# Two-layer sparse-attention trunk on one core: first gate summed by VectorE, compression's products and the second layer's values in longer runs, second scale and shift in four column tiles

## The chip, the core and the metric

The kernel runs on one core of one Trainium2 chip. TensorE (PE in the profile; PEld is its weight load), VectorE (DVE), ScalarE (ACT), GpSimd (POOL) and the queue engine SyncE (SP) each run their own queue of instructions in order and wait for each other by semaphores. The metric is the device time of one execution in microseconds (us), lower is better.

## The reference

Two transformer blocks over x (256 tokens, 1024 wide). c is one row of 1024 numbers; it gives each layer a shift, a scale and a gate. Layer 0 uses `nsa_mixer` (three attention branches, one of them over compressed blocks), layer 1 uses `moba_mixer` (with 256 tokens it is one causal attention). Everything is float32.

```python
cond = silu(c)
for i in range(2):
    shift, scale, gate = split(cond @ ada_w[i] + ada_b[i], 3)          # 1024 -> 3 x 1024
    h = rms_norm(x, norm_g[i]) * (1 + scale) + shift
    y = nsa_mixer(h, ...) if i == 0 else moba_mixer(h, ...)
    x = x + gate * y
# in nsa_mixer, for keys (i = 0) and values (i = 1):
#   flat: 15 blocks x 4 heads of 32 tokens x 64 = 2048 numbers each
#   gelu(flat @ cmp_w1[i] + cmp_b1[i]) @ cmp_w2[i]                     # cmp_w1: 2048 x 256
# attention, per head: softmax(q @ k.T * scale, causal) @ v;  y = (o * silu(z)) @ w_out
```

## The kernel before

Weights come through SP's queue into 128x1024 buffers (`early`, then six `raw`). Large products are made of two halves: ScalarE rounds a weight piece to float32r (`hi`), VectorE subtracts it from the piece (`lo`), and TensorE adds hi.hi, hi.lo and lo.hi. HT holds the normed input, KTA the keys, VA the values, qg the queries, GT the gated outputs. Small sums are plain float32; each is two instructions of TensorE in the trace.

The program is written in its natural order, and a planner (`Plan.issue`) sets the real one: it keeps a clock for each engine, picks the ready operation that can start first, then by level and by key, and allots buffers. Two tables move single operations by hand: `LATER_BY` shifts keys (operation numbers), `HOLD` gives an earliest start in planned ns. Operations recorded in one `plan.group()` are issued together. All recorded operations carry the line of the issuing helper (L404), so the profile's groups go by tile names.

Some products use column tiles: with `tile_position=(0, 32*j)` a product with 32 output rows takes a quarter of the array's columns, with `(0, 64*e)` a half, and products in different tiles run side by side. The four places that matter here:

- `ada_rows` / `ada_gate(0)`: the first layer's gate row is cond @ ada_w, 16 products of 32 rows x 512 columns in four column tiles (`ps<-raw,condz`), spread to all partitions by two products with ones (`ps<-row,ones`). `ada_gate(1)` does the second one on VectorE (`gate<-raw,condz,gate`, 8 sums of 128x1024) and spreads it by two full-width products (`ps<-gate,ones`).
- `ada_ss(1, 0, 4)` and `ada_ss(1, 4, 4)`: the second layer's scale and shift, 16 such products each, then four transposes each (`ps<-identF,row`).
- `cmp_steps`: the compression's products, 16 groups of two products of 64 rows x 256 columns (`ps<-p,p`), one half of the columns for keys and one for values. Its weights lie in `p` buffers.
- `values`, called by `pair_b` for each of the second layer's eight head pairs (`ps<-pT,VA`).

The first three are handed out as side work: `beside()` takes a step of the list `side` between steps of the attention.

Of the kernel before, what the change touches and what calls it, by code (L numbers as in the profile page):

```python
# [1 line left out]

# [12 lines left out]
OP = mybir.AluOpType  # L15
AX = mybir.AxisListType

P = 128
S = 256
D = 1024  # L20
HEADS = 16
KVH = 4
HD = 64
# [11 lines left out]

TICK = 10240 / 3
DEEP = 2e4
TILED, LATER, PAUSE = -0.5, 0, 93.0
SHORT_ROWS, SMALL, BEHIND, EARLY_RATE = 1.1, 7e4, 5500.0, 348.0
ISSUE, FIRST_BYTE, RATE, LANDED = 450.0, 1500.0, 315.0, 700.0  # L40

LATER_BY = [
# [12 lines left out]
]  # L55
SHIFT = {i: d for a, b, d in LATER_BY for i in range(a, b + 1)}
HOLD = {
    29: 2400, 32: 3700, 33: 3700, 51: 7200, 312: 35600, 391: 48800, 1276: 152700, 1340: 169100, 1350: 168000,
    1415: 182100, 1573: 197400, 1576: 198800, 1579: 197400, 1585: 198700, 1636: 205200, 1655: 209300,
}  # L60


# [10 lines left out]
class Plan:  # L73
# [120 lines left out]
    def _cost(self, engine, method, args, kw, aps):  # L194
        def free(a):
            n = 1
            for _, k in a.ap[1:]:
                n *= k
            return n

        if "dma" in method:
            self.bytes = free(aps[0]) * aps[0].shape[0] * 4
            if aps[1].shape[-1] <= 128 and self.bytes > 1e5:
                self.bytes *= SHORT_ROWS
            if self.bytes <= 1e5:
                self.bytes += SMALL
            return max(ISSUE, self.bytes / RATE) if engine == "S" else ISSUE
        psum = any(str(a.space).endswith("PSUM") for a in aps)
        n = max(free(a) for a in aps)
        if engine == "T":  # L210
            if method == "transpose":
                return 262.0 if aps[1].dtype == F32 else 180.0
            cols = free(aps[2])
            if aps[2].dtype == F32:
                m, rows = free(aps[1]), aps[1].shape[0]
                if "tile_position" in kw and m * rows <= 64 * P:
                    return max(cols * 4.28 * max(32, m) / P * max(32, rows) / P, 60.0) + (100.0 if rows < P else 0.0)
                return 2 * max(cols * 2.14, 264.0)
            return max(cols * (1.07 if aps[2].dtype == F32R else 1.0), 264.0)
        if engine == "A":  # L220
            return 0.833 * n + (51.0 if psum else 94.0) + 93.0 * sum(isinstance(kw.get(k), bass.AP) for k in ("bias", "scale", "accum_out"))
        if engine == "G":
            return 1.5 * n + 270.0
        if method == "reciprocal":
            return 6.5 * n + 68.0
        fast = not psum and (method == "tensor_copy" or method.startswith("tensor_scalar"))
        pointers = len(aps) - 2 if method.startswith("tensor_scalar") else 0
        return (0.521 if fast else 1.042) * n + 68.0 + 61.0 * pointers
# [22 lines left out]
    def issue(self, opening=()):  # L251
# [51 lines left out]
        while done < len(ops):  # L303
            best = None
            for e, ops_e in ready.items():
# [4 lines left out]
                for op in ops_e:  # L310
# [4 lines left out]
                    for n in op["needs"]:  # L315
# [4 lines left out]
                        t = max(t, r)  # L320
# [41 lines left out]
            if e == "T":  # L362
                tick = int(start // TICK)
                if op["mode"] != mode:
                    cost += 240.0
                mode = op["mode"]
                cost = cost * (1 / 2.4 if tally.get(tick - 1, 0.0) >= 3060.0 else 1 / 1.2)
                tally[tick] = tally.get(tick, 0.0) + op["cost"]
                if (start + cost) // TICK > tick:
                    cost += PAUSE  # L370
# [61 lines left out]
def kernel(  # L432
# [39 lines left out]
        late["pool"] = ctx.enter_context(tc.tile_pool(name="attn", bufs=1))  # L472

    KP = 2
    W1_HOME = ("p", "p")
    SPINS = 8
    START = [("s", 2, 2), ("k", 1), ("s", 4, 2), ("k", 2), ("s", 6, 2), ("k", 3)]
    plan.tag("acc", psum, 512, 2, space="PSUM")
# [155 lines left out]
    def load(src, tag="raw"):  # L634

        t = tile_of(tag, *src.shape[1:])
        with plan.at(CHAIN):
            Q.dma_start(t, src)
        return t
# [54 lines left out]
    def ada_ss(l, k0, nk, loaded=None):  # L694
# [23 lines left out]
        V.scalar_tensor_tensor(a_, a_, 1.0, RT[:, ROW_G + 8 * l + k0:ROW_G + 8 * l + k0 + nk], op0=OP.add, op1=OP.mult)  # L718
        V.tensor_add(b_, tv[:, :, 0], RT[:, b:b + nk])

    gates_of = {}

    def ada_gate(l):

        gate = gates_of[l] = tile_of("gate", D)
        bias = bass.AP(tensor=ada_b.tensor, offset=ada_b.offset + l * 3 * D + 2 * D, ap=[[D, 1], [1, D]])
        if l:
            G.memset(gate, 0.0)
            Q.dma_start(gate[0:1], bias)
            for kk in range(8):  # L730
                w = ada_piece(l, kk, 2 * D, D)[:, 0, :]
                with plan.at(FILL):
                    V.scalar_tensor_tensor(gate, w, condz[:, kk, 0:1], gate, op0=OP.mult, op1=OP.add)
                yield
            mix, src = (ones, ones), (gate[:, 0:512], gate[:, 512:1024])
        else:
            g = yield from ada_rows(l, (2 * D, 2 * D + 512), 512)
            for s in range(2):
                Q.dma_start(g[64 * s + 1:64 * s + 2], bias[:, s * 512:(s + 1) * 512])
            ts = [tile_of("ps", 512) for s in range(2)]  # L740
            with plan.at(FILL):
                with plan.group():
                    for s in range(2):
                        T.matmul(ts[s], ones[64 * s:64 * s + 64], g[64 * s:64 * s + 64], start=True, stop=True,
                                 tile_position=(64 * s, 0))
                for s in range(2):
                    A.copy(gate[:, s * 512:(s + 1) * 512], ts[s])
            return
        for s in range(2):
            t = tile_of("ps", 512)  # L750
            with plan.at(FILL):
                T.matmul(t, mix[s], src[s], start=True, stop=True)
                A.copy(gate[:, s * 512:(s + 1) * 512], t)

    side = []
# [177 lines left out]

    def values(o, parts, first):

        with plan.group():
            for n, (v, pT) in enumerate(parts):
                for e in range(2):
                    T.matmul(o[64 * e:64 * e + 64, 0:S], v[0], pT[e][:, 0:S], start=(first and n == 0), stop=False,
# [252 lines left out]
    def cmp_steps(hid):  # L1192

        for kq in range(4):
            for k in range(4):
                if k % 2 == 0:
                    w1 = [load(bass.AP(tensor=nsa_cmp_w1.tensor, offset=nsa_cmp_w1.offset + (kv * 2048 + kq * 512 + k * P) * 256,
                                       ap=[[256, P], [P * 256, 2], [1, 256]]), W1_HOME[kv]) for kv in range(2)]
                with plan.at(FILL), plan.group():
                    for kv in range(2):  # L1200
                        T.matmul(hid[64 * kv:64 * kv + 64, 0:256],
                                 FLAT[kv][kq // 2][:, 4 * (kq % 2) + k].rearrange("p g n -> p (g n)"), w1[kv][:, k % 2, :],
                                 start=(kq == 0 and k == 0), stop=(kq == 3 and k == 3), tile_position=(0, 64 * kv))
            if kq < 3:
                yield

    hid = tile_of("ps", 512)
    side += [cmp_steps(hid), ada_gate(0), ada_ss(1, 0, 4), ada_ss(1, 4, 4)]
    QT = qt_tiles()
    gates = const.tile([P, 2, HEADS, 3], F32, name="gates")  # L1210

# [267 lines left out]
    def pair_b(i):  # L1479
# [12 lines left out]
        for m in range(2):  # L1492
            for e in range(2):
                V.tensor_scalar_mul(pm[m][:, e], pm[m][:, e], sm[:, m, e:e + 1])
        pT = p_transposed(lambda e, j: pm[0][:, e] if j == 0 else pm[1][:, e, (j - 1) * P:j * P])
        o = tile_of("ps", 512)
        vs = slice(g * HD, (g + 1) * HD)
        values(o, [([VB[:, m, vs] for m in range(2)], pT)], True)
        gated(i, o, zT[i])

    for i in range(8):
        pair_b(i)
        beside()
    assert not side

    def done_b(m, sl, acc):
# [34 lines left out]
```

## Time and profile before

| | us |
|---|---|
| median of 3 runs | 313.22 (312.3 to 313.4) |
| profiled execution | 312.48 |
| its span, first to last instruction | 310.7 |
| TensorE busy | 301.6 |
| VectorE busy | 242.0 |
| ScalarE busy | 205.1 |

Roughly, 0 to 60 us are the head and the first products, 60 to 110 the queries and the compression, 110 to 190 the first layer's attention, 190 to 200 its output, 200 to 250 the second layer's input products, 250 to 290 its attention, and the rest its output. A matmul's start is sharp in this trace, its end is modelled: the time that a run of matmuls takes is read from its start to the start of what follows.

### The profile page before, as it was taken

The numbers are of one execution on the slowest core, as the hardware profiler recorded it, in microseconds if no ns is written. First come the engines' busy times: TensorE is split into PE (matmuls) and PEld (weight loads), VectorE is DVE, ScalarE is ACT, GpSimd is POOL, SyncE is SP. The second block draws the span as 40 slices with busy tenths as digits, with TensorE's granted clock in tenths as the row PEclk, the third lists the DMA queues.
The fourth block names the chain that finished last, engine by engine and source line by source line (L and its number), as shares of the span: only waits on it lengthen the run. The fifth ranks groups of instructions, "written<-read, shape, count | busy, mean of one in ns | idle before, by whom it ended". The sixth has DMA issues, their size and how long they took to land.

```text
span 310.7 us, 6167 instructions
## 1 busy us (share of the span) xinstructions
PE 301.6 (97%) x2133; PEld 242.0 (78%) x2133; DVE 242.0 (78%) x734; ACT 205.1 (66%) x486; POOL 28.2 (9%) x99
## 2 busy tenths in 40 slices
PE   4999999999999999999999999999999999999995
PEld 4765677768767687976798887787788999987784
DVE  4763483658997399963999989796799999999465
ACT  4735254784845566964999993795585599988520
POOL 8038950000000000000000000000000000000000
PEclk9999999999999999999999999999999999999999
DMA  8999999749999890948925429236288760740002
GB/s 249 321 356 368 366 356 319 223 139 307 331 294 333 282 345 6 329 145 290 309 80 186 153 72 307 96 77 198 69 289 273 225 231 9 263 136 2 0 35 103
DMA packets 44174, 65.82 MB, mean 212 GB/s; under 512 B 4221, under 2 KB 20971, under 8 KB 44142
## 3 DMA queue, kind: packets, MB, share of 16 engines
q1 hardware_dynamic: 43782, 65.36, 64.3%
q8 instruction: 17, 0.28, 0.4%
q14 instruction: 15, 0.12, 0.1%
q10 hardware_dynamic: 168, 0.06, 0.1%
q0 software_dynamic: 192, 0.00, 0.0%
HBM read 64.36 MB, written 1.05 MB: 211 GB/s over the span
## 4 chain that ended last, share of the span: by engine, by line
PE 90%; DVE 3%; DMA 3%; ACT 2%; issue 1%; ACTq 0%; SPq 0%; DVEq 0%
PE ps L404 52%; PE acc L404 38%; DMA y<-in_ada_b_dram 2%; DMA early<-in_nsa_w_in_dram 1%; ACT hi L404 1%; DVE lo L404 1%; DVE rs L404 1%; DVE y L404 0%; ACT n_parts L404 0%; ACTq L404 0%; DVE X L404 0%; DVE p L404 0%; ACT n_out L404 0%; ACT HT L404 0%; DVE n_parts L404 0%
## 5 line engine op out<-in xcount | busy, mean ns | idle before, releaser
L404 ACT CAST hi<-raw 128x1024 fp32r<-128x1024 f32 (+1 forms) x48 | 48.6, 1021 | 24.3 <-PE acc L404 16.5
L404 DVE TENSOR_TENSOR lo<-raw,hi 128x1024 fp32r<-128x1024 f32 (+1 forms) x48 | 56.5, 1182 | 6.5 <-ACT hi L404 6.3
L404 PE MATMUL acc<-hi,HT 128*128 128x512 f32 (+1 forms) x160 | 49.6, 382 | 0.1
L404 ACT ACTIVATE p<-p,tiny 128x128 f32<-128x128 f32 (+1 forms) x96 | 42.9, 451 | 6.5 <-DVE tiny L404 6.2
L404 PE MATMUL acc<-HT,hi 128*128 128x256 f32 x192 | 37.4, 285 | 0.0
L404 DVE CUSTOM_DVE_ANT_0 p<-ps,causal 128x128 f32<-128x128 f32 (+1 forms) x96 | 30.6, 346 | 8.2 <-ACT hi L404 5.6
L404 PEld LDWEIGHTS acc<-hi,HT 128*128 128x128 f32 x160 | 29.1, 188 | 8.0 <-issue 2.5
L404 PEld LDWEIGHTS acc<-HT,hi 128*128 128x128 f32 x192 | 30.2, 189 | 0.5 <-issue 0.5
L404 PE MATMUL acc<-lo,HT 128*128 128x512 f32 (+1 forms) x80 | 30.3, 383 | 0.2
L404 PE MATMUL ps<-hi,HT 128*128 128x512 f32 (+1 forms) x96 | 28.2, 365 | 0.0
L404 PE MATMUL acc<-HT,lo 128*128 128x256 f32 x96 | 27.2, 284 | 0.0
L404 PE MATMUL ps<-KTA,qg 128*128 128x256 f32 (+2 forms) x192 | 26.9, 281 | 0.0
L404 PEld LDWEIGHTS ps<-KTA,qg 128*128 128x128 f32 x192 | 24.0, 189 | 2.7 <-issue 1.7
L404 ACT COPY pT<-ps 128x384 f32<-128x384 f32 x48 | 21.0, 477 | 4.0 <-PE ps L404 4.0
L404 ACT CAST hi<-early 128x1024 fp32r<-128x1024 f32 (+2 forms) x17 | 14.9, 896 | 13.1 <-DMA early<-in_nsa_w_in_dram 8.9
L404 PE MATMUL ps<-hi,qg 128*128 128x256 f32 (+1 forms) x96 | 23.4, 326 | 0.0
L404 DVE TENSOR_TENSOR lo<-early,hi 128x1024 fp32r<-128x1024 f32 (+2 forms) x17 | 17.6, 1047 | 5.9 <-ACT hi L404 5.9
L404 PE MATMUL acc<-hi,qg 128*128 128x512 f32 x64 | 21.7, 405 | 0.0
L404 PE MATMUL ps<-identF,p 128*128 128x128 f32 x144 | 21.2, 274 | 0.0
L404 PEld LDWEIGHTS ps<-hi,HT 128*128 128x128 f32 x96 | 17.0, 188 | 3.5 <-issue 1.2
L404 PEld LDWEIGHTS ps<-identF,p 128*128 128x128 f32 x144 | 16.8, 141 | 2.7 <-issue 0.7
L404 PE MATMUL ps<-pT,VA 128*64 128x256 f32 (+1 forms) x192 | 18.5, 333 | 0.0
(220 smaller groups left out, 614.4 us busy)
## 6 DMA issues: line engine op xcount, KB each, us to landing
raw<-in_ada_w_dram SPq DMA_DIRECT2D x32, 512.0 KB, 5.2
raw<-in_moba_w_in_dram SPq DMA_DIRECT2D x20, 512.0 KB, 4.4
early<-in_ada_w_dram SPq DMA_DIRECT2D x12, 512.0 KB, 9.5
raw<-in_nsa_w_in_dram SPq DMA_DIRECT2D x12, 512.0 KB, 6.8
early<-in_nsa_w_in_dram SPq DMA_DIRECT2D x9, 512.0 KB, 8.8
p<-in_nsa_cmp_w_dram SPq DMA_DIRECT2D x16, 256.0 KB, 4.1
raw<-in_nsa_w_out_dram SPq DMA_DIRECT2D x8, 512.0 KB, 4.8
raw<-in_moba_w_out_dram SPq DMA_DIRECT2D x8, 512.0 KB, 5.2
```

The lines of the kernel that those rows point to most:

```text
L404: r = getattr(self.engines[e], method)(*[self._real(a) for a in args], **{k: self._real(a) for k, a in kw.items()})
```

## The change

`ada_gate` now takes the second layer's way for both layers: 8 sums on VectorE and two full-width products with ones. A new `ada_all` computes the second layer's scale and shift with four column tiles (shift low, shift high, scale low, scale high) over eight weight rows, and transposes once. `cmp_steps` loads four weight pieces, two of them into `zT` buffers, and issues eight products in one group. The second layer's pairs go two at a time, with their values in one group. The side list becomes compression, second scale and shift, first gate. The planner's costs for tiled products change, and both tables are new.

```diff
-TILED, LATER, PAUSE = -0.5, 0, 93.0
+TILED, LATER, PAUSE, SWITCH = -0.5, 0, 93.0, 440.0
...
 LATER_BY = [
-    (162, 162, -17), (329, 337, -24), (338, 338, 30), (344, 351, -111), (359, 366, -38), (372, 372, -38),
+    (110, 111, -64), (256, 256, 155), (308, 311, -51), (317, 318, -56), (331, 331, 298), (351, 351, 26),
...
-                    cost += 240.0
+                    cost += SWITCH
...
-    W1_HOME = ("p", "p")
+    W1_HOME = ("p", "zT")
...
+    def ada_all():
+
+        acc = tile_of("ps", 512)
+        for kk in range(8):
+            w = [ada_piece(1, kk, c0, D)[:, 0] for c0 in (0, D)]
+            with plan.at(FILL), plan.group():
+                for s in range(2):
+                    for h in range(2):
+                        j = 2 * s + h
+                        T.matmul(acc[32 * j:32 * j + 32], condz[:, kk], w[s][:, 512 * h:512 * h + 512],
+                                 start=(kk == 0), stop=(kk == 7), tile_position=(0, 32 * j))
+            if kk < 7:
+                yield
+        g = tile_of("row", 512)
+        A.copy(g, acc)
+        t = tile_of("ps", 512)
+        with plan.group():
+            for q in range(4):
+                T.transpose(t[:, q * P:(q + 1) * P], g[:, q * P:(q + 1) * P], identF)
...
     def ada_gate(l):
...
-        if l:
-            G.memset(gate, 0.0)
-            Q.dma_start(gate[0:1], bias)
-            for kk in range(8):
-                w = ada_piece(l, kk, 2 * D, D)[:, 0, :]
-                with plan.at(FILL):
-                    V.scalar_tensor_tensor(gate, w, condz[:, kk, 0:1], gate, op0=OP.mult, op1=OP.add)
-                yield
-            mix, src = (ones, ones), (gate[:, 0:512], gate[:, 512:1024])
-        else:
-            g = yield from ada_rows(l, (2 * D, 2 * D + 512), 512)
...
+        G.memset(gate, 0.0)
+        Q.dma_start(gate[0:1], bias)
+        for kk in range(8):
+            w = ada_piece(l, kk, 2 * D, D)[:, 0, :]
             with plan.at(FILL):
...
+                V.scalar_tensor_tensor(gate, w, condz[:, kk, 0:1], gate, op0=OP.mult, op1=OP.add)
+            yield
         for s in range(2):
             t = tile_of("ps", 512)
             with plan.at(FILL):
-                T.matmul(t, mix[s], src[s], start=True, stop=True)
+                T.matmul(t, ones, gate[:, s * 512:(s + 1) * 512], start=True, stop=True)
...
-    side += [cmp_steps(hid), ada_gate(0), ada_ss(1, 0, 4), ada_ss(1, 4, 4)]
+    side += [cmp_steps(hid), ada_all(), ada_gate(0)]
...
-    for i in range(8):
-        pair_b(i)
+    for i in range(0, 8, 2):
+        pairs = [pair_b(i)]
         beside()
+        pairs.append(pair_b(i + 1))
+        beside()
+        values_b(pairs)
```

What it moves shows in the order of each engine's instructions. First, TensorE near the first step of the compression. Before, four compression products (`ps_204<-p,p`) are followed by four of the first gate (`ps_158<-raw,condz`), and then by the second query chunk's:

```order
L404 MATMUL ps_215<-hi_258,HT 128x512
L404 MATMUL ps_204<-p_716,p_714 64x256
L404 MATMUL ps_204<-p_732,p_722 64x256
L404 MATMUL ps_204<-p_716,p_714 64x256
L404 MATMUL ps_204<-p_732,p_722 64x256
L404 MATMUL ps_158<-raw_649,condz 32x512
L404 MATMUL ps_158<-raw_665,condz 32x512
L404 MATMUL ps_158<-raw_649,condz 32x512
L404 MATMUL ps_158<-raw_665,condz 32x512
L404 MATMUL acc_273<-hi_349,HT 128x304
```

After, at the same place, with weights in `p` and in `zT` buffers:

```order
L406 MATMUL ps_153<-hi_297,HT 128x256 x2
L406 MATMUL ps_246<-p_718,p_716 64x256
L406 MATMUL ps_246<-p_734,p_722 64x256
L406 MATMUL ps_246<-p_718,p_716 64x256
L406 MATMUL ps_246<-p_734,p_722 64x256
L406 MATMUL ps_246<-zT_714,p_716 64x256
L406 MATMUL ps_246<-zT_736,p_722 64x256
L406 MATMUL ps_246<-zT_714,p_716 64x256
L406 MATMUL ps_246<-zT_736,p_722 64x256
L406 MATMUL ps_207<-raw_644,condz 32x512 x2
L406 MATMUL ps_207<-raw_658,condz 32x512 x2
L406 MATMUL acc_272<-hi_243,HT 128x304
```

Eight compression products stand together where four did, and the four 32-row products behind them are now the first of the second scale and shift. Over the whole kernel the compression's runs were of 4, 4, 4, 4, 4, 8 and 4 products and are now of 8, 8 and 16; the 32x512 products stood in runs of 4, 4, 4, 8, 12, 8, 4 and 4 and now stand in runs of 4, 12, 8, 4 and 4.

Second, VectorE in the first layer's attention. Before, near the third gated product (`g<-zT,ps`), between the masked maxima (`ISA p,tiny<-ps,causal`) and the scaling of p:

```order
L404 ISA p_732,tiny_1251<-ps_215,causal 128x256
L404 ISA tiny_1251 128x1
L404 SCALAR_TENSOR_TENSOR g_1214<-zT_729,ps_204 128x256
L404 RECIPROCAL tiny_904<-tiny_904 128x8
L404 SCALAR_TENSOR_TENSOR tiny_904<-tiny_904,gates 128x4 x2
L404 TENSOR_TENSOR p_725<-p_725,tiny_904 128x512
L404 TENSOR_SCALAR p_722<-p_722,tiny_904 128x256 x2
```

After, near the second gated product:

```order
L406 ISA p_734,tiny_1010<-ps_246,causal 128x128
L406 ISA tiny_1010 128x1
L406 SCALAR_TENSOR_TENSOR gate_171<-raw_637,condz,gate_171 128x1024
L406 SCALAR_TENSOR_TENSOR g_1022<-zT_714,ps_173 128x256
L406 SCALAR_TENSOR_TENSOR gate_171<-raw_610,condz,gate_171 128x1024
L406 TENSOR_TENSOR qg_1521<-g_1022,qg_1521 128x256
L406 SCALAR_TENSOR_TENSOR gate_171<-raw_616,condz,gate_171 128x1024
L406 TENSOR_TENSOR AB_115<-ps_198,RT 128x8 x2
```

Three of the first gate's eight sums stand here; the other five follow before the sixth gated product. Between the first and the last run of values in this layer, TensorE now has 132 products of the 256-column z kind (`acc<-HT,hi` and `acc<-HT,lo`) where it had 51.

Third, TensorE at the second layer's values (`ps<-pT,VA`). Before, part of the longest run, in which three head pairs follow each other (`ps_158`, `ps_242`, `ps_215`); its first two rows are left out:

```order
L404 MATMUL ps_158<-pT_1458,VA 64x128
L404 MATMUL ps_158<-pT_1328,VA 64x128
L404 MATMUL ps_242<-pT_1351,VA 64x256
L404 MATMUL ps_242<-pT_1344,VA 64x256
L404 MATMUL ps_242<-pT_1351,VA 64x128
L404 MATMUL ps_242<-pT_1344,VA 64x128
L404 MATMUL ps_215<-pT_1363,VA 64x256
L404 MATMUL ps_215<-pT_1328,VA 64x256
L404 MATMUL ps_215<-pT_1363,VA 64x128
L404 MATMUL ps_215<-pT_1328,VA 64x128
L404 MATMUL ps_152<-KTA,qg_1487 128x256 x4
```

After, the first of four runs of two pairs each:

```order
L406 MATMUL ps_207<-KTA,qg_1296 128x256 x4
L406 MATMUL ps_246<-pT_1419,VA 64x256
L406 MATMUL ps_246<-pT_1403,VA 64x256
L406 MATMUL ps_246<-pT_1419,VA 64x128
L406 MATMUL ps_246<-pT_1403,VA 64x128
L406 MATMUL ps_173<-pT_1410,VA 64x256
L406 MATMUL ps_173<-pT_1415,VA 64x256
L406 MATMUL ps_173<-pT_1410,VA 64x128
L406 MATMUL ps_173<-pT_1415,VA 64x128
L406 MATMUL acc_272<-HT,hi_342 128x256 x2
```

The eight pairs stood in runs of 1, 3, 2 and 2 pairs and stand in runs of 2, 2, 2 and 2.

## Rows read from the trace of the kernel before

**Rows 1.** The page: busy us of each engine (share of the span) and instructions, and the chain that ended last, by engine.

```profile
PE 301.6 (97%) x2133; PEld 242.0 (78%) x2133; DVE 242.0 (78%) x734; ACT 205.1 (66%) x486; POOL 28.2 (9%) x99
...
PE 90%; DVE 3%; DMA 3%; ACT 2%; issue 1%; ACTq 0%; SPq 0%; DVEq 0%
```

**Rows 2.** TensorE's waits: in total, times, longest.

```profile
PE ps L404 <- DMA rot<-in_c_dram: 2.9, 1, 2.9
...
PE ps L404 <- DVE p L404: 0.5, 1, 0.5
```

**Rows 3.** Stages (us from the span's start): length, then busy us and instructions of PE, PEld, DVE, ACT and POOL, granted clock, DMA share, GB/s.

```profile
100.00:150.00 50.00, 50.00 (x434) 38.10 (x433) 34.72 (x159) 32.85 (x103) 0.00 (x0) 1.00 0.70 241
150.00:188.00 38.00, 37.99 (x305) 32.55 (x306) 36.58 (x135) 36.53 (x105) 0.00 (x0) 1.00 0.48 151
...
250.00:290.00 40.00, 40.00 (x327) 35.42 (x327) 38.04 (x151) 35.10 (x105) 0.00 (x0) 1.00 0.34 109
```

**Rows 4.** TensorE's timeline around a lone run of compression products: start, us to the modelled end, what.

```profile
72.85 0.30 PE L404 MATMUL acc<-lo,HT 128*128 128x304 f32 x1
73.07 1.08 PE L404 MATMUL ps<-p,p 128*64 128x256 f32 x8
74.09 0.41 PE L404 MATMUL acc<-hi,HT 128*128 128x304 f32 x1
74.33 0.30 PE L404 MATMUL acc<-lo,HT 128*128 128x304 f32 x1
74.47 0.30 PE L404 MATMUL acc<-hi,HT 128*128 128x304 f32 x1
```

**Rows 5.** The same around the one double run, with the first gate's and the second scale's products behind it, and 256-column z products ahead of it.

```profile
101.05 0.39 PE L404 MATMUL acc<-HT,hi 128*128 128x256 f32 x2
101.28 0.28 PE L404 MATMUL acc<-HT,lo 128*128 128x256 f32 x1
101.48 1.95 PE L404 MATMUL ps<-p,p 128*64 128x256 f32 x16
103.36 1.92 PE L404 MATMUL ps<-raw,condz 128*32 128x512 f32 x16
105.22 0.39 PE L404 MATMUL ps<-KTA,qg 128*128 128x256 f32 x1
```

**Rows 6.** The same at the first eight 32-row instructions.

```profile
68.27 1.07 PE L404 MATMUL ps<-raw,condz 128*32 128x512 f32 x8
69.26 0.41 PE L404 MATMUL acc<-hi,HT 128*128 128x304 f32 x1
```

**Rows 7.** The same at the first gate's spread over the partitions.

```profile
108.97 1.13 PE L404 MATMUL ps<-row,ones 64*128 64x512 f32 x4
110.03 0.44 PE L404 MATMUL ps<-identF,g 128*128 128x128 f32 x2
```

**Rows 8.** The same at the second gate's two.

```profile
281.90 1.10 PE L404 MATMUL ps<-gate,ones 128*128 128x512 f32 x2
282.93 1.52 PE L404 MATMUL ps<-pT,VA 128*64 128x256 f32 x16
...
285.96 1.02 PE L404 MATMUL ps<-gate,ones 128*128 128x512 f32 x2
286.82 0.49 PE L404 MATMUL ps<-identF,p 128*128 128x128 f32 x3
```

**Rows 9.** The same at one of the two sets of transposes of the second scale and shift.

```profile
128.92 0.62 PE L404 MATMUL ps<-identF,row 128*128 128x128 f32 x4
129.38 0.38 PE L404 MATMUL ps<-identF,p 128*128 128x128 f32 x2
```

**Rows 10.** The same at the second layer's values: the run of three pairs.

```profile
270.65 2.37 PE L404 MATMUL ps<-pT,VA 128*64 128x256 f32 x24
272.95 0.50 PE L404 MATMUL ps<-KTA,qg 128*128 128x256 f32 x2
```

**Rows 11.** The same at the first layer's scale and shift: one run that takes longer than the others, and a lone one (512-column products follow each other at 0.23).

```profile
23.61 1.52 PE L404 MATMUL ps<-early,condz 128*32 128x256 f32 x16
25.07 0.50 PE L404 MATMUL acc<-hi,HT 128*128 128x512 f32 x1
...
33.52 0.39 PE L404 MATMUL ps<-lo,HT 128*128 128x512 f32 x1
33.75 0.39 PE L404 MATMUL ps<-hi,HT 128*128 128x512 f32 x1
34.07 1.07 PE L404 MATMUL ps<-early,condz 128*32 128x256 f32 x16
35.07 0.51 PE L404 MATMUL ps<-hi,HT 128*128 128x512 f32 x1
```

**Rows 12.** VectorE's timeline at the first and the last sum of the second gate; in brackets, idle time before it and what released it.

```profile
216.64 1.28 DVE L404 SCALAR_TENSOR_TENSOR gate<-raw,condz,gate 128x1024 f32<-128x1024 f32 x1 [2.19 <-DMA raw<-in_ada_w_dram]
...
280.47 1.28 DVE L404 SCALAR_TENSOR_TENSOR gate<-raw,condz,gate 128x1024 f32<-128x1024 f32 x1
281.67 0.41 DVE L404 CUSTOM_DVE_ANT_0 p<-ps,causal 128x256 f32<-128x256 f32 x1
```

**Rows 13.** One stretch, columns as in rows 3: from the start of the first gated product of the first layer to that of the sixth.

```profile
138.50:176.72 38.22, 38.22 (x320) 30.08 (x316) 31.95 (x128) 32.66 (x100) 0.00 (x0) 1.00 0.61 197
```

**Rows 14.** The page: loads of the compression's weights, size of one, and us from issue to landing.

```profile
p<-in_nsa_cmp_w_dram SPq DMA_DIRECT2D x16, 256.0 KB, 4.1
```

More of the change, by code (lines that the diff above doesn't have):

```diff
@@ L1 @@
-from contextlib import ExitStack, contextmanager
+from contextlib import ExitStack, contextmanager, nullcontext
 import concourse.bass as bass
@@ L57 @@
 HOLD = {
-    29: 2400, 32: 3700, 33: 3700, 51: 7200, 312: 35600, 391: 48800, 1276: 152700, 1340: 169100, 1350: 168000,
-    1415: 182100, 1573: 197400, 1576: 198800, 1579: 197400, 1585: 198700, 1636: 205200, 1655: 209300,
[3 rows of a table added]
 }
@@ L216, in _cost @@
                 if "tile_position" in kw and m * rows <= 64 * P:
-                    return max(cols * 4.28 * max(32, m) / P * max(32, rows) / P, 60.0) + (100.0 if rows < P else 0.0)
+                    if rows < P:
+                        return max(cols * 2.02 * max(32, m) / P, 269.0)
+                    return max(cols * 4.03 * max(32, m) / P, 60.0)
                 return 2 * max(cols * 2.14, 264.0)
@@ L719, in ada_ss, with rt @@
         V.tensor_add(b_, tv[:, :, 0], RT[:, b:b + nk])
+    def ada_all():
[16 more added lines that the diff above has]
+                T.transpose(t[:, q * P:(q + 1) * P], g[:, q * P:(q + 1) * P], identF)
+        tv = t.rearrange("p (q s h z) -> p s h q z", q=4, s=2, h=2)[:, :, :, :, 0]
+        a_, b_ = (AB[1][:, s].rearrange("p (h q) -> p h q", h=2) for s in range(2))
+        def rt(at):
+            return RT[:, at:at + 8].rearrange("p (h q) -> p h q", h=2)
+        V.tensor_add(a_, tv[:, 1], rt(ROW_ADA + 32))
+        V.scalar_tensor_tensor(a_, a_, 1.0, rt(ROW_G + 8), op0=OP.add, op1=OP.mult)
+        V.tensor_add(b_, tv[:, 0], rt(ROW_ADA + 24))
     gates_of = {}
@@ L726, in ada_gate @@
         bias = bass.AP(tensor=ada_b.tensor, offset=ada_b.offset + l * 3 * D + 2 * D, ap=[[D, 1], [1, D]])
-        if l:
-            G.memset(gate, 0.0)
-            Q.dma_start(gate[0:1], bias)
-            for kk in range(8):
-                w = ada_piece(l, kk, 2 * D, D)[:, 0, :]
-                with plan.at(FILL):
-                    V.scalar_tensor_tensor(gate, w, condz[:, kk, 0:1], gate, op0=OP.mult, op1=OP.add)
-                yield
-            mix, src = (ones, ones), (gate[:, 0:512], gate[:, 512:1024])
-        else:
-            g = yield from ada_rows(l, (2 * D, 2 * D + 512), 512)
-            for s in range(2):
-                Q.dma_start(g[64 * s + 1:64 * s + 2], bias[:, s * 512:(s + 1) * 512])
-            ts = [tile_of("ps", 512) for s in range(2)]
-            with plan.at(FILL):
[L742 to L748, printed above, removed]
+        G.memset(gate, 0.0)
+        Q.dma_start(gate[0:1], bias)
+        for kk in range(8):
+            w = ada_piece(l, kk, 2 * D, D)[:, 0, :]
+            with plan.at(FILL):
+                V.scalar_tensor_tensor(gate, w, condz[:, kk, 0:1], gate, op0=OP.mult, op1=OP.add)
+            yield
         for s in range(2):
@@ L934, in values @@
     def values(o, parts, first):
-        with plan.group():
+        with nullcontext() if plan.open else plan.group():
             for n, (v, pT) in enumerate(parts):
@@ L1194, in cmp_steps @@
         for kq in range(4):
[L1195 to L1199, printed above, removed]
+            w1 = [[load(bass.AP(tensor=nsa_cmp_w1.tensor, offset=nsa_cmp_w1.offset + (kv * 2048 + kq * 512 + k * P) * 256,
+                                ap=[[256, P], [P * 256, 2], [1, 256]]), W1_HOME[k // 2]) for kv in range(2)] for k in (0, 2)]
+            with plan.at(FILL), plan.group():
+                for k in range(4):
                     for kv in range(2):
                         T.matmul(hid[64 * kv:64 * kv + 64, 0:256],
-                                 FLAT[kv][kq // 2][:, 4 * (kq % 2) + k].rearrange("p g n -> p (g n)"), w1[kv][:, k % 2, :],
+                                 FLAT[kv][kq // 2][:, 4 * (kq % 2) + k].rearrange("p g n -> p (g n)"), w1[k // 2][kv][:, k % 2, :],
                                  start=(kq == 0 and k == 0), stop=(kq == 3 and k == 3), tile_position=(0, 64 * kv))
@@ L1494, in pair_b, with values_b @@
                 V.tensor_scalar_mul(pm[m][:, e], pm[m][:, e], sm[:, m, e:e + 1])
[L1495 to L1499, printed above, removed]
-    for i in range(8):
-        pair_b(i)
+        return i, p_transposed(lambda e, j: pm[0][:, e] if j == 0 else pm[1][:, e, (j - 1) * P:j * P])
+    def values_b(pairs):
+        os = [tile_of("ps", 512) for _ in pairs]
+        with plan.group():
+            for o, (i, pT) in zip(os, pairs):
+                values(o, [([VB[:, m, i // 2 * HD:(i // 2 + 1) * HD] for m in range(2)], pT)], True)
+        for o, (i, _) in zip(os, pairs):
+            gated(i, o, zT[i])
+    for i in range(0, 8, 2):
+        pairs = [pair_b(i)]
         beside()
+        pairs.append(pair_b(i + 1))
+        beside()
+        values_b(pairs)
     assert not side
```

24 rows, old and new, of tables (HOLD, LATER_BY) are left out of this document.

## The prediction

> **What bounds the kernel now.** I read the page first, then the waits of TensorE, then a table by stage, then TensorE's own timeline, because the first three all point there. TensorE is busy 97% of the span and the chain that ended last is 90% TensorE [rows 1]. Its longest single wait behind the head of the program is 0.5 us [rows 2]. The stage table shows it without a gap from 100 to 290 us, while VectorE has room in 100:150 and little in 150:188 (36.58 of 38 us) and 250:290 [rows 3]. The granted clock is 1.00 (2.4 GHz) in each of these stretches. So a microsecond taken from TensorE's queue is a microsecond of the kernel, as long as VectorE keeps up in 130 to 190 us.
>
> A busy TensorE says nothing of what its time buys, and that is where this change acts. The column-tiled runs are read best from start to start. A run of eight compression matmuls goes from 73.07 to 74.09, 1.02 us. The 304-column product ahead of it starts 0.22 before it and the one behind takes 0.24, where such products follow each other at 0.14 [rows 4]. So a lone run of eight costs 1.02 + 0.08 + 0.10 = 1.20 us. Sixteen go from 101.48 to 103.36, 1.88 us [rows 5], so eight more cost 0.86. A lone run of any length thus pays about 0.34 us on top: 0.18 at its borders and some 0.15 at its start. Where a run of another tile shape follows at once, only the 0.15 is paid again: the 32-column products take 1.86 for sixteen and 0.99 for eight [rows 5, 6].
>
> **The change, part by part.**
>
> *First gate and compression (one sum, since their runs are interleaved).* Before, the place holds eight eights of compression in seven runs, five eights of 32-column products in four runs, and the gate's row-tiled spread over partitions, 1.06 us [rows 7], all in seven separate stretches. By the numbers above: 8 x 0.86 + 7 x 0.15 = 7.93; 5 x 0.86 + 4 x 0.15 = 4.90; 1.06; 7 x 0.18 = 1.26; together 15.15 us. After, by the order, it is eight eights of compression in three runs, one eight of 32-column products, three stretches: 7.33 + 1.01 + 0.54 = 8.88. That is 6.27 less. The other seven eights (second scale and shift) stand later in both, as 24, 16, 8 and 8; after has one stretch more, +0.18. Net **-6.1**. Of this 4 x 0.86 = 3.4 is the gate's four eights, which VectorE now adds up.
>
> *The gate's spread over partitions becomes two full-width sums with ones.* The trace has two of the same kind for the second gate: 1.03 and 0.86 us [rows 8]. **+1.9**.
>
> *Second scale and shift.* One row of four column tiles instead of two halves with two partial sums each: as many tiled matmuls, but four transposes fewer, 128.92 to 129.38 [rows 9]: **-0.5**. Two of ScalarE's copies and two small VectorE reductions go too, off the chain.
>
> *Second layer's values.* The doubled runs bring next to nothing: the order of before already had runs of one, three, two and two pairs, that is four runs, and after has four of two. Three pairs in one run take 2.30 [rows 10], 0.77 each, so a start more or less is all that is at stake. **-0.1**, and this part of the change does not do what it says.
>
> *First layer's scale and shift.* Not edited, but the new table joins four stretches of sixteen to two. A lone one takes 1.00 and 0.09 ahead of it [rows 11]; a joint saves the two borders and a start, about 0.34 as above. But one such run took 1.46 instead of 1.00, waiting for its second load [rows 11], so a joined run may wait as long. Bounds 0 and -0.7; I take the far one, since 40 us of work behind it can slide: **-0.7**.
>
> The sum on TensorE is -6.1 + 1.9 - 0.5 - 0.1 - 0.7 = **-5.5 us**.
>
> *Eight gate sums on VectorE.* One takes 1.28 us, 1.20 from its start to the next instruction's [rows 12], so +9.6 us. The order puts all eight between the first and the sixth gated product of the first layer. Before, that stretch runs from 138.50 to 176.72 and VectorE is busy 31.95 of 38.22 us [rows 13]: room 6.27, so 3.3 us do not fit if all else stays. But the cover has grown: between the first and the last values run of the layer, the order has 132 of the z products (256 columns) where before had 51. At 0.115 each [rows 5] that lengthens TensorE's own work there by 81 x 0.115 = 9.3 us, taken from ahead of the stretch. Bounds: 0 (all hidden) and +3.3. I take **+0.5**, near the first, because TensorE has more to do there than VectorE; without that cover it is the 3.3.
>
> *Compression weights in the zT buffers.* Those buffers hold the compression's inputs until they are transposed. Between the second buffer's transposes and its first use, TensorE's queue has 12 products at 0.23, 10 at 0.115, 8 transposes at 0.115 and an eight, about 5.7 us. A load takes 4.1 us to land [rows 14] and half a microsecond to issue. It fits by about 1 us, so 0; if it lands later, TensorE waits in order, with the second query chunk behind it.
>
> *Loads.* Bytes are the same. The gate's sums keep raw buffers until VectorE has read them, which belongs to the rivals.
>
> So -5.5 + 0.5 = **-5.0**. The profiled execution took 312.48 (span 310.7 and 1.8 around it), which gives 307.5; it lies 0.7 under the median of the runs, 313.22, so I predict **308.2**.
>
> **The rivals.**
>
> *VectorE becomes the bound in the first layer's attention.* For it: 36.58 of 38 us in 150:188, and ScalarE as full, 36.53 [rows 3]. Each softmax step there goes TensorE, VectorE, ScalarE, VectorE, TensorE, so a sum of 1.2 us in front of a step delays the transposes by as much once TensorE has no filler. Against it: the z products moved in. If half of the room is lost as well, about 3 to 4 us come back: 310 to 312.5.
>
> *Slower: a gate sum reaches the head of VectorE's queue before its load has landed.* Rows show it once for the second gate: VectorE idle for 2.19 us, released by the load [rows 12]; there it cost nothing, since TensorE had products to do. Now the sums stand between mask, maximum and scaling steps on which the transposes wait. One late load costs up to 2.2 us; from the third on (6.6) the gain is gone; with four, 312.48 - 5.5 + 8.8 = 315.8, by the median 316.5. Against it: DMA share is 0.48 in 150:188 [rows 3], so the wires are free, and only the release of the six raw buffers could hold a load up. The Trainium skill (TensorE: Matmul & The Clock Gate, "Architectural detail: the array is 16× 32×32, not 1× 128×128") says VectorE's queue is strictly first in, first out, which speaks against putting loads' consumers among softmax steps: by it nothing behind such a sum could pass, and the time would be that of this rival. The trace agrees so far as the one row goes.
>
> *The new table as a whole.* It reorders every engine, the head included: c is now the fifth load on ScalarE's queue. Nothing in rows prices this; I allow 2 us to either side.
>
> **How the numbers follow.** The measurement cannot tell less than about 0.5% (1.6 us) from no change. Chances: the forecast, 306.5 to 310, 0.60; more, under 306.5, by the table, 0.08; VectorE takes part back, 310 to 312.5, 0.20, of it 0.09 over 0.5% faster and 0.11 within; slower by late loads or sums, 0.11; a change hidden wholly for another reason, 0.01. So faster 0.77, same 0.12, slower 0.11. The range 305.0 to 312.5 leaves out the slow case and the far end of the fast one; the likeliest case's own is 306.5 to 310.
>
> **What would show it.** Right: three compression runs of 16, 16 and 32 instructions at 1.88, 1.88 and about 3.6 us; two 128x512 sums with ones more, under 1.1 us each; TensorE's longest wait behind the head still under 1 us; TensorE busy near 296 us where it was 301.6 [rows 1]. Wrong: VectorE idle before a gate sum, released by a load; TensorE waiting on p or pT for microseconds between 130 and 190; TensorE waiting for zT near 66 us.

## The result, and the profile after

The changed kernel took 309.80 us (308.65 to 309.89) beside 313.12 for the kernel before, a ratio of 0.988 (95% interval 0.986 to 0.990). A second timing, on another occasion, gave 308.84 beside 313.17, 0.986 (0.983 to 0.988). That is 3.3 and 4.3 us less: **faster by 1.2 to 1.4%**, inside the predicted range and 0.6 to 1.6 us above the predicted 308.2. The profiled execution took 308.65 where before's took 312.48; its span is 306.9 us where before's is 310.7.

The page of the kernel after, busy time and the chain that ended last, against [rows 1]:

```profile
PE 297.4 (97%) x2097; PEld 242.4 (79%) x2097; DVE 248.6 (81%) x737; ACT 203.0 (66%) x484; POOL 29.3 (10%) x100
PE 83%; DVE 5%; ACT 5%; DMA 3%; issue 2%; ACTq 1%; DVEq 0%
```

TensorE's busy time fell by 4.2 us and it is still the bound, at the same 97%, though the chain that ended last runs through VectorE and ScalarE for 10% of the span where it was 5%. Its waits (total, times, longest), against [rows 2]:

```profile
PE ps L406 <- DMA X<-in_x_dram: 4.3, 1, 4.3
PE ps L406 <- DMA rot<-in_c_dram: 0.8, 1, 0.8
PE acc L406 <- DVE lo L406: 0.2, 1, 0.2
```

Behind the head there is one of 0.2 us. The two stages of the first layer's attention, against [rows 3] (busy time of each engine, granted clock, DMA share):

```profile
100.00:150.00 50.00, 49.79 (x430) 40.44 (x431) 46.00 (x192) 39.57 (x129) 0.00 (x0) 1.00 0.66 234
150.00:188.00 38.00, 38.00 (x277) 31.39 (x276) 35.29 (x97) 30.98 (x79) 0.00 (x0) 1.00 0.62 196
```

VectorE took on 9.6 us of sums there, all of it before 163 us, and TensorE idles 0.21 us in all. The gate sums of both layers, from the page (busy, mean ns, idle before them):

```profile
L406 DVE SCALAR_TENSOR_TENSOR gate<-raw,condz,gate 128x1024 f32<-128x1024 f32 x16 | 20.4, 1276 | 0.4 <-DMA raw<-in_ada_w_dram 0.4
```

All sixteen together waited 0.4 us for their loads. In before one of them alone waited 2.19 [rows 12]. The rival of late loads did not come.

TensorE's own timeline where the compression now runs:

```profile
66.38 1.08 PE L406 MATMUL ps<-p,p 128*64 128x256 f32 x8
67.29 1.03 PE L406 MATMUL ps<-zT,p 128*64 128x256 f32 x8
68.25 1.06 PE L406 MATMUL ps<-raw,condz 128*32 128x512 f32 x8
69.25 0.41 PE L406 MATMUL acc<-hi,HT 128*128 128x304 f32 x1
...
72.74 1.14 PE L406 MATMUL ps<-p,p 128*64 128x256 f32 x7
73.66 0.38 PE L406 MATMUL ps<-zT,p 128*64 128x256 f32 x1
73.71 0.38 PE L406 MATMUL ps<-p,p 128*64 128x256 f32 x1
73.87 1.08 PE L406 MATMUL ps<-zT,p 128*64 128x256 f32 x7
74.89 0.41 PE L406 MATMUL acc<-lo,HT 128*128 128x304 f32 x1
...
81.86 1.08 PE L406 MATMUL ps<-p,p 128*64 128x256 f32 x8
82.77 1.03 PE L406 MATMUL ps<-zT,p 128*64 128x256 f32 x8
83.63 1.03 PE L406 MATMUL ps<-p,p 128*64 128x256 f32 x8
84.50 1.03 PE L406 MATMUL ps<-zT,p 128*64 128x256 f32 x8
85.46 0.50 PE L406 MATMUL acc<-hi,HT 128*128 128x512 f32 x1
```

From start to start the compression's runs take 1.87 (to 68.25), 2.15 and 3.60 us and the 32-column eight 1.00: 8.62, where the forecast's prices, without borders, give 8.34. The 0.28 more is all in the middle run; why is not settled. (In the kernel with cut runs below, the two halves of that run take 1.01 each, so there the excess is gone.)

### The profile page after: what moved, and what is told of

It is laid out like the page before. It is cut to its first block, busy times and chain, and to the rows that moved or that the text cites. A ratio compares the mean times of both kernels' runs of the same rounds, so it can differ in the third digit from the quotient of the medians.

```text
span 306.9 us, 6115 instructions
## 1 busy us (share of the span) xinstructions
PE 297.4 (97%) x2097; PEld 242.4 (79%) x2097; DVE 248.6 (81%) x737; ACT 203.0 (66%) x484; POOL 29.3 (10%) x100
## 4 chain that ended last, share of the span: by engine, by line
PE 83%; DVE 5%; ACT 5%; DMA 3%; issue 2%; ACTq 1%; DVEq 0%
PE ps L406 48%; PE acc L406 36%; DVE p L406 3%; ACT p L406 2%; DMA rot<-in_c_dram 1%; DMA raw<-in_nsa_w_out_dram 1%; DVE lo L406 1%; ACT pT L406 1%; ACT hi L406 1%; ACTq L406 1%; ACT n_out L406 1%; DVE tiny L406 0%; ACT qg L406 0%; DVE n_out L406 0%; ACT y L406 0%
## 5 line engine op out<-in xcount | busy, mean ns | idle before, releaser
L406 PE MATMUL acc<-HT,hi 128*128 128x256 f32 x192 | 39.0, 288 | 0.0
L406 PE MATMUL ps<-hi,HT 128*128 128x512 f32 (+1 forms) x96 | 28.9, 367 | 0.0
L406 PE MATMUL ps<-hi,qg 128*128 128x256 f32 (+1 forms) x96 | 24.4, 324 | 0.0
L406 PE MATMUL acc<-hi,qg 128*128 128x512 f32 x64 | 23.3, 415 | 0.0
L406 DVE SCALAR_TENSOR_TENSOR gate<-raw,condz,gate 128x1024 f32<-128x1024 f32 x16 | 20.4, 1276 | 0.4 <-DMA raw<-in_ada_w_dram 0.4
```

The costliest lines, as they stand in the source:

```text
L406: r = getattr(self.engines[e], method)(*[self._real(a) for a in args], **{k: self._real(a) for k, a in kw.items()})
```

## The experiments

They ask four things: what a microsecond on TensorE's queue and a cut run cost; whether VectorE's sums are hidden, and by what; what the late load of c costs; and how much belongs to the edit and how much to the new table. Unless it is said otherwise, an experiment alters only what is handed out behind the planner, so the planned order stays.

**TensorE's price.**

```
+            if op["id"] in tiled:          # the first of ada_all's eight groups
+                for _ in range(4):
+                    emit(e, [(m, args, {**kw, "stop": True}) for m, args, kw in op["calls"]])
             emit(e, op["calls"])
```

> The kernel after with the first of its eight groups of 128x512 column-tiled products for the second scale and shift run five times instead of once (the first four results are overwritten): as many tiled products more as the old gate had, in one joined run, all data there. Theory (a microsecond on TensorE's queue is a microsecond of the kernel, and an eight costs 0.86): each four products here last as long as eight of the old ones or as a 32-column eight of 256 columns, so 4 x 0.86 = 3.4 us longer than the kernel after. Rival (part of TensorE's time in this stretch is slack that other work fills): under 2 us.

Measured 312.33 us, ratio 0.998 (0.996 to 0.999): 2.5 and 3.5 us over the two timings of the kernel after. TensorE's timeline of it shows the price to the digit:

```profile
69.45 4.50 PE L306 MATMUL ps<-raw,condz 128*32 128x512 f32 x40
```

Forty take 4.50 us where eight show 1.06 above: 32 more in 3.44, 0.86 for each eight. The whole rose by 3 us within half a microsecond, so TensorE's queue is paid about one for one. That fits the 3.4 us that the forecast put on the four eights of the old gate.

**Cut runs.** The second half of a group follows one ordinary product later (in the first group the 32-column eight goes between as well):

```
+            if op["id"] in halves:         # 4 groups of compression, 4 of values
+                kept = op
+                emit(e, op["calls"][:len(op["calls"]) // 2])
```

> The kernel after with eight of its column-tiled runs cut in halves, the second half one ordinary product later: the four groups of eight compression products and the second layer's four groups of two pairs' values. No work is added. Theory (a lone run costs 0.34 us over its products, 0.18 at its borders and 0.15 at its start): the compression's four cuts 4 x 0.34 = 1.4, the values' four cuts 4 x (0.80 + 0.80 - 1.45 + 0.18) = 1.3: 2.7 us longer than the kernel after. Rival (borders and starts are hidden by the products around them): under 0.7 us.

Measured 311.32 us, ratio 0.9935 (0.991 to 0.996); 2.5 us over the kernel after on the same chip (308.84). The timeline of the cut kernel at the values of the second layer:

```profile
263.83 0.87 PE L306 MATMUL ps<-pT,VA 128*64 128x256 f32 x8
264.63 0.38 PE L306 MATMUL acc<-HT,hi 128*128 128x256 f32 x1
264.94 0.87 PE L306 MATMUL ps<-pT,VA 128*64 128x256 f32 x8
265.74 0.39 PE L306 MATMUL acc<-HT,hi 128*128 128x256 f32 x1
```

Each half takes 0.80; uncut, the same sixteen take 1.45. In the compression only three cuts took effect: the third group's second half joined the fourth group. So 3 x 0.34 + 1.3 = 2.3 us were to come, and 2.5 came. The borders and starts of tiled runs are real time, not hidden by their neighbours: some 0.34 us for one more run. The Trainium skill (TensorEngine Tiling (Array Packing), "Key Properties") says that a change of tiling mode drains TensorE. The 2.5 us for seven cuts agree with it.

**The sums on VectorE.** First more of them, then almost none:

```
             emit(e, op["calls"])
+            if op["id"] in sums:           # the eight sums of the first gate
+                _, (gate, w, _, _), kw = op["calls"][0]
+                emit(e, 1 * [("scalar_tensor_tensor", (gate, w, 0.0, gate), kw)])
```

> The kernel after with a second VectorE instruction of the same size behind each of the eight sums of the first gate (the same weights times 0.0, so the result does not change): 9.6 us more on VectorE in the first layer's attention, nothing moved on any engine. Theory (the sums cost nothing because TensorE has more to do there than VectorE): under 1 us over the kernel after. Rival (VectorE is the bound in that stretch, and the change paid for part of the sums already): 5 to 9.6 us longer, a loss against before.

With `2 *` for `1 *`:

> The kernel after with two more VectorE instructions of the same size behind each of the eight sums of the first gate (the same weights times 0.0): 19.2 us more on VectorE. Theory (cover by TensorE's own products, some 9 us of it): the first 9.6 us cost under 1 us, of the second 9.6 most is paid: 3 to 9 us over the kernel after. Rival one (no cover): 15 to 19 us longer. Rival two (room for it everywhere): under 1 us.

And the sums themselves cut to 32 columns, which leaves the rest of the first gate out:

```
-                emit(e, op["calls"])
+                m, (gate, w, c, _), kw = op["calls"][0]
+                emit(e, [(m, (gate[:, 0:32], w[:, 0:32], c, gate[:, 0:32]), kw)])
```

> The kernel after with each of the eight gate sums cut to 32 of its 1024 columns, so the first gate is wrong in the other columns: some 9 us less on VectorE, every instruction, load and wait still there. Doubling the sums was paid in full, 1 us for 1 us, so what is asked is on which side of its limit VectorE stands with the sums as they are. Theory (the sums just fit, and TensorE is the bound with them): within 0.5 us of the kernel after. Rival one (the forecast's far bound, 3.3 us do not fit): 1.5 to 3.3 us shorter, which would be the whole of what the change fell short. Rival two (VectorE is the bound outright): up to 9 us shorter.

Doubled: 320.41 us, ratio 1.023 (1.020 to 1.026). Threefold: 331.63, 1.060 (1.056 to 1.063). Cut to 32 columns: 308.21, 0.984 (0.981 to 0.987), beside 308.84 for the kernel after on the same chip. So the sums as they are cost about 0.6 us, a difference that the two intervals do not tell from none, and every further microsecond of VectorE there costs 1.1 to 1.2. That is over the rivals' bounds of 9.6 and 19 us too. My theory of a cover of some 9 us on top fell: the cover ends where the sums end. TensorE's two largest waits with doubled sums, which the kernel after has not:

```profile
PE ps L306 <- DVE g L306: 3.2, 2, 2.4
PE ps L306 <- DVE tiny L306: 2.9, 3, 2.1
```

Then what hid the first 9.6 us? The same eight instructions were put into the kernel before, whose TensorE still does the old gate:

```
+                emit("V", [("scalar_tensor_tensor", (X[:, 0], X[:, 1], 0.0, X[:, 0]), dict(op0=OP.mult, op1=OP.add))])
```

In the first of two such runs they stand at the counts of VectorE's instructions read off the trace:

> The kernel before with eight VectorE instructions of the gate sums' size and form (the residual plus 0.0 times its other half, so the result does not change) put among the softmax steps of the first layer's attention, at the places where the kernel after has its sums; TensorE keeps its old gate. 9.6 us more on VectorE, nothing taken from TensorE. Theory (the forecast's: the room of that stretch is 6.27 us, and the 81 z products moved in by the change are the cover for the rest): 3.3 us longer than before. Rival one (TensorE waits in full for each, as for the doubled sums of the kernel after): 8 to 10 us longer. Rival two (there was room without the moved products): under 1 us.

In the second at places told by the gated products:

> The kernel before with eight VectorE instructions of the gate sums' size again (the result does not change), now at the places that the sums have in the kernel after by the gated products: three around the second product, two behind the third, three between the fourth and the fifth, which in the profile of before is 141 to 166 us. In the run with eight such instructions that was meant to have these places they had come at 155 to 179 us. Theory (the forecast's account: VectorE's room there is 6.27 us, the rest shows without the z products moved in): 3.3 us longer than before. Rival one (the room is at 140 to 150 us alone, where VectorE is busy 4.38 us of 10, and 150 to 180 us has none: the first five are free, the last three are paid): 3 x 1.2 = 3.7 us, with TensorE waiting at 160 to 170 us alone. Rival two (each pushes the softmax steps behind it, the room is lost too): 8 us longer.

The first gave 320.88 us, ratio 1.027 (1.022 to 1.031), about 8 us longer; but its sums had slipped to 155 to 195 us (six start by 179.31, the last two at 191.42 and 193.34; the expectation above counts the six), so it says only that there is no room at those places. The second had them at 142 to 165 us and gave 319.08, ratio 1.022 (1.019 to 1.024): some 6.4 us over before. No expectation met it: it is more than 3.3 and 3.7 and less than 8. Before, by tens of microseconds from 130 to 170 (third figure VectorE, after PE and PEld), and then the same kernel with the sums:

```profile
130.00:140.00 10.00, 10.00 (x91) 7.79 (x89) 6.76 (x35) 6.96 (x24) 0.00 (x0) 1.00 0.54 195
140.00:150.00 10.00, 10.00 (x92) 6.68 (x89) 4.38 (x18) 5.84 (x17) 0.00 (x0) 1.00 0.94 317
150.00:160.00 10.00, 9.99 (x88) 9.20 (x88) 10.00 (x50) 9.72 (x32) 0.00 (x0) 1.00 0.67 210
160.00:170.00 10.00, 10.00 (x84) 8.48 (x83) 10.00 (x30) 9.69 (x27) 0.00 (x0) 1.00 0.39 121
```

```profile
140.00:150.00 10.00, 10.00 (x93) 6.89 (x90) 7.60 (x18) 5.23 (x15) 0.00 (x0) 1.00 0.96 321
150.00:160.00 10.00, 9.26 (x68) 8.09 (x68) 10.00 (x35) 8.64 (x23) 0.00 (x0) 0.83 0.63 200
160.00:170.00 10.00, 7.75 (x61) 6.51 (x60) 10.00 (x38) 7.11 (x28) 0.00 (x0) 1.00 0.02 7
```

Before, VectorE's room lies at 130 to 150 us, 5.6 us of it behind 140; from 150 on it is full. Four of the eight sums lie at 142 to 150 us and a fifth starts at its end, some 5 us of work, but that slice rises by 3.2 us alone: the rest only pushes the softmax steps into the full stretch. TensorE then waits 3.0 us at 150 to 170. The kernel after in the same four slices, and then the one with its sums cut to 32 columns:

```profile
130.00:140.00 10.00, 10.00 (x93) 7.95 (x91) 9.31 (x34) 8.41 (x27) 0.00 (x0) 1.00 0.66 247
140.00:150.00 10.00, 9.79 (x84) 8.47 (x84) 10.00 (x43) 9.26 (x36) 0.00 (x0) 1.00 0.65 234
150.00:160.00 10.00, 10.00 (x87) 9.00 (x86) 10.00 (x35) 7.38 (x24) 0.00 (x0) 1.00 0.60 185
160.00:170.00 10.00, 10.00 (x72) 7.93 (x71) 10.00 (x32) 8.35 (x29) 0.00 (x0) 1.00 0.77 245
```

```profile
130.00:140.00 10.00, 10.00 (x94) 7.96 (x92) 6.95 (x37) 8.48 (x28) 0.00 (x0) 1.00 0.72 254
140.00:150.00 10.00, 10.00 (x88) 8.85 (x86) 8.65 (x43) 9.79 (x38) 0.00 (x0) 1.00 0.71 256
150.00:160.00 10.00, 10.00 (x86) 9.06 (x87) 9.75 (x36) 7.54 (x22) 0.00 (x0) 1.00 0.63 196
160.00:170.00 10.00, 10.00 (x74) 8.03 (x72) 7.35 (x29) 8.54 (x28) 0.00 (x0) 1.00 0.62 212
```

VectorE is busy 39.3 us of 40 with the sums and 32.7 with the sums cut, where it was 31.1 before. So the new order has no more room in these 40 us than the old one (7.3 us and 8.9); its room lies elsewhere: 2.65 us of it in the last slice, and VectorE is busy 8.55 us of 170 to 180 behind it, where before's is full until 180. The attention also starts earlier: the compression ends at 85.46 us instead of 103.36 [rows 5], the first run of values starts at 119.6 instead of 136.9, and the first gated product at 128.4 instead of 138.50. The earlier values do not need the new table: in the two kernels without tables below they start at 121.5 and 136.4. That this order hides the sums is shown for the order as it is; that the earlier start is what does it is read from these rows, since no run moved it alone. Nor did any run put the sums into the kernel before at 133 to 138 us, where three of them stand in the kernel after and before has 3.2 us of room.

**The load of c at the head.**

In the kernel after, c's load is handed out ahead of the loop over all operations, and left out inside it:

```
+        emit("A", ops[0]["calls"])
         done = 0
         while done < len(ops):
```

> The kernel after with one move: the load of c is handed out first on ScalarE's queue, as before the change, and the four loads of the table R behind it; every other instruction keeps its place. Theory (the late load of c is a real loss at the head): TensorE's first product on c starts near 2.9 us instead of 7.1, the first product of the layer near 12.6 instead of 13.3, and the whole gets 0.7 to 1.3 us shorter than the kernel after: a span of 305.6 to 306.2 us, a ratio to before of 0.984 to 0.986. Rival (the head waits for the loads of R and of the inputs anyway, and each of R's loads is now later by one place): within 0.3 us of the kernel after.

In the kernel before, it is handed out behind the last of R's loads (`moved`):

```
+            if op["id"] == moved:
+                emit("A", ops[0]["calls"])
```

> The kernel before with c's load put behind the four loads of the table R on ScalarE's queue, as the kernel after has it; nothing else moves. Theory (the late load of c is paid at the head): 0.7 to 1.3 us longer than before, ratio 1.002 to 1.004. Rival (TensorE's loss at the head is caught up at 44 us, where it waits for VectorE if it comes there early, as in the kernel after with c's load first): within 0.3 us of before.

Late in the kernel before: 315.07 us, ratio 1.006 (1.004 to 1.009), 1.9 us longer. Early in the kernel after: 308.91, ratio 0.987 (0.985 to 0.989), not to be told from the kernel after. The same move is worth 1.9 us in one order and nothing that shows in the other. The waits point to the new table's other move, the products on X ahead of the one on c, which no run took back alone. TensorE's waits at the head, of before with c late and of after with c first:

```profile
PE ps L304 <- DMA rot<-in_c_dram: 7.1, 1, 7.1
```

```profile
PE ps L306 <- DMA X<-in_x_dram: 4.3, 1, 4.3
PE acc L306 <- DVE HT L306: 0.7, 1, 0.7
```

With c first the layer's first product comes at 12.93 us instead of 13.30 (12.57 in before), so 0.37 is won at the head, no more than the two profiles of the kernel after differ there (13.30 and 13.70); then TensorE waits 0.7 at 44 us. VectorE's row there, and GpSimd's beside it:

```profile
42.82 1.32 DVE L306 TENSOR_SCALAR rot<-n_out,AB 128x256 f32<-128x256 f32 x1
```

```profile
43.05 0.95 POOL L306 MEMSET gate<- 128x1024 f32 x1
```

The same VectorE instruction takes 0.45 us at 40.67. Here it lasts until just after the memset ends, and that memset is the first gate's, which the change added. In the profile of the kernel after the two miss each other (43.04 for 0.51 us, and 44.08). The Trainium skill (Trainium Architecture — The Big Picture, "What this means for kernel authors") says that VectorE and GpSimd share a port pair under an exclusive lock, which would explain it; no run took the memset away.

**Edit or table.**

```
-LATER_BY = [ ... ]   -HOLD = { ... }
+LATER_BY = []        +HOLD = {}
```

> The kernel before with both tables of numbers that shift the planner's order emptied, so its plain rules set the order: slower than before, by how much no row tells; it is the baseline of the next one.

> The kernel after with both tables emptied. Against the kernel before without its tables this is the edit without the new order. Theory (the gain is the edit's: 6.1 - 1.9 + 0.5 + 0.1 - 0.5 on VectorE): 4.3 us, within 1.5, shorter than the kernel before without tables. Rival (the gain is the new table's, and the plain rules put the sums where TensorE waits for them): same or longer.

316.40 us (ratio 1.012, 1.008 to 1.016) and 311.70 (0.995, 0.994 to 0.997): the edit alone, the planner's new costs included, is worth 4.7 us, near the 4.3 expected; by the first interval it could be a microsecond more or less. Before's tables are worth 3.4 us, after's 1.9 to 2.9. So the gain is the edit's, and the plain rules find an order for the sums as well.

> The kernel after, unchanged, beside the next three on the same chip, to have their baseline from the same hour: 309.8 us, ratio to before 0.988.

This is the second timing given above.

## Why the prediction was right, point by point

- **Right: the bound and the price.** TensorE's queue is paid about one for one (3 us for 3.44 added), and the 0.34 us of a lone tiled run held in the cuts (2.5 against 2.3).
- **Gate and compression, -6.1:** 0.28 less came, by the middle run: -5.8.
- **Two sums with ones, +1.9:** as forecast in effect. A pair starts 0.56 us before the next product, but that product then holds the queue for 0.63 to 0.69 where such products follow each other at 0.23: 1.0 us for a pair.
- **Second scale and shift, -0.5:** one set of transposes stands where two did; the one left takes 0.39 from start to start.
- **Scale and shift of the first layer, -0.7:** the joints came as sized, but a wait went that the forecast left standing. Two runs of 32 now take 1.86 each:

```profile
24.53 1.93 PE L406 MATMUL ps<-early,condz 128*32 128x256 f32 x32
26.39 0.51 PE L406 MATMUL ps<-hi,HT 128*128 128x512 f32 x1
...
37.00 1.93 PE L406 MATMUL ps<-early,condz 128*32 128x256 f32 x32
38.86 0.50 PE L406 MATMUL ps<-lo,HT 128*128 128x512 f32 x1
```

  The four before took 1.46 and three times 1.00 [rows 11], and two borders of 0.18 went: 4.46 + 0.36 - 3.72 = 1.1. Of this 0.64 is the two joints (0.34 each were forecast) and 0.46 the wait for a second load.
- **Values of the second layer, -0.1:** four runs at 1.45, 5.8 us, are 0.2 less than before's four. That this part of the change does not do what it says was right.
- **Sums on VectorE, +0.5:** the number was right (0 to 0.6), but by luck: its account was wrong in two places. The step "room 6.27, so 3.3 us do not fit if all else stays" took busy time as if it could be moved: put into before's order at 142 to 165 us, the sums cost some 6.4 us, not 3.3, because they push the softmax steps into slices that are full already. And the cover of 9.3 us counted in z products is not there on top: doubled sums were paid in full. What hides the single ones is the new order as a whole; which part of it is not shown.
- **The table's head, "2 us to either side":** the mechanism was named and left without a price. Its bare price is 1.9 us, and by the waits it is X ahead of c in the same table that takes most of it back: TensorE's waits at the head went from 2.9 + 1.0 to 4.3 + 0.8 us, and the layer's first product came 0.73 later. In the second timing's profile it came 1.13 later, so the term is 0.7 to 1.1. It is the one that was missing from the sum.
- **The sum.** With these sizes it is -5.8 + 1.9 - 0.5 - 0.2 - 1.1 + 0.7 = -5.0, where the profile shows -3.8 and the medians -3.3 and -4.3. That it equals the forecast's -5.0 is luck: the head was left out, the wait at the first scale and shift was kept in, and these nearly cancel. The 0 to 0.6 of the sums on VectorE is not in it and may be part of the 1.2 us between the terms and the profile. The rest is open: no wait shows it, so it may lie in how TensorE's products follow each other where the table gave them other neighbours, or in the spread of the runs.

The signs that the forecast named came: runs of 1.87, 2.15 and 3.60 us, no wait over 0.2 behind the head, TensorE busy 297.4 where about 296 was said.

## What to carry to other kernels

Where one engine's queue is the bound, price an edit by start-to-start times on that queue, and count a tiled run's entry and exit with its products. Before moving work to a second engine, ask not how much idle time it has in a stretch but where that time lies and what stands behind the new work; the slices of the stretch tell, the sum over it does not. A late load costs what the first instruction that needs it holds up, so look at the order behind it before pricing the load.

## What the hardware showed that was not expected

A short wait of TensorE can come with a fall of its granted clock that costs more than the wait. The kernel before with the early sums, by 2 us:

```profile
148.00:150.00 2.00, 2.00 (x20) 1.82 (x16) 1.97 (x7) 2.00 (x7) 0.00 (x0) 1.00 1.02 344
150.00:152.00 2.00, 1.26 (x7) 0.69 (x7) 2.00 (x5) 2.00 (x4) 0.00 (x0) 0.71 0.97 333
152.00:154.00 2.00, 2.00 (x11) 2.00 (x11) 2.00 (x7) 1.60 (x3) 0.00 (x0) 0.50 0.42 160
154.00:156.00 2.00, 2.00 (x18) 1.87 (x16) 2.00 (x6) 1.91 (x3) 0.00 (x0) 0.94 0.12 16
```

TensorE waits twice at 150 to 152, 0.35 us and 0.38, and the clock falls from 1.00 to 0.50 (2.4 to 1.2 GHz) between the two, by 151, and is back by 156. Ahead of the fall TensorE ran eleven narrow products (`ps<-KTA,qg`, 128x32) and, behind the first wait, its first transposes. At full speed the lost clock is 2 x 0.29 + 2 x 0.50 + 2 x 0.06 = 1.7 us, more than twice the waits. Longer waits, 0.94 us up to 162.26 and 1.31 up to 167.35, left it at 1.00, so a wait alone does not settle it; what does is not shown. With 3.1 us of waiting the lost clock makes 4.8 of the 5.5 us by which this profile's span is longer than before's. In the profile with doubled sums the clock fell once as well, behind the wait of 2.4 us (0.84 at 170 to 180 us, 1.6 us lost). That is about what the doubled sums cost beyond their own 9.6 us.
